# Softmax on one core: eight transfers of 3 to 25 rows in place of ten, five-row scaling of the late tiles, a later test for the general path

## The chip, the cores and the metric

One core of one Trainium2 chip. The metric is device time in microseconds, the median of several executions. All executions told of here were in the fast state (granted clock 1.0), so they are compared with each other. Executions of the kernel before agree within 0.3%; the effects below are about 1% or less, so every experiment was timed in five rounds.

## The reference

```
x: [16, 1024, 512] float32
x_scaled = x / 2.0
exp_x = exp(x_scaled - max(x_scaled, axis=-1))
out = exp_x / sum(exp_x, axis=-1)
```

The kernel takes exp without subtracting the maximum and counts afterwards whether every row's sum lies in a safe range. If not, a general path with the maximum runs over all data. For this input it doesn't run, but its test does.

## The kernel before

There are 16384 rows of 512 floats, 128 rows for each partition. A "row" below is one such row in all 128 partitions: 256 KB. Everything works in place in an arena of 98 rows, so the last 30 rows must wait until stores have freed room. ScalarE issues loads, SyncE issues stores.

```python
TILES = [(3, 0), (5, 3), (15, 8), (15, 23), (15, 38), (15, 53), (15, 68), (15, 83), (15, 0), (15, 15)]  # rows, place
LATE = {8: (0, 1, 2), 9: (3,)}   # tile 8 waits for the stores of 0, 1, 2; tile 9 for that of 3
TURN = 83                        # ScalarE issues the late loads after the exps of 83 rows
...
# VectorE: chunks of five rows, two together where a tile has two left
for j, ks in enumerate(pairs):
    nc.vector.reciprocal(...)._wait_ge(s_exp, ks[-1] + 1).then_inc(s_rec, 1)
    nc.vector.tensor_mul(...)._wait_ge(s_rec, j + 1).then_inc(s_mul, 1)
...
# SyncE: a store waits for the last scaling of its tile
def store(eng, t):
    eng.wait_ge(s_mul, upto[t])
    eng.dma_start(out=dram(of, t), in_=sb(t)).then_inc(stored_by.get(t, s_end), 16)
...
# VectorE, ScalarE and GpSimd: the test for the general path
def rounds(eng, body, step=1):
    eng.wait_ge(s_flag, 1)
    eng.reg_load(i, flag[0:1, 0:1])
    with eng.While(lambda: eng.snap(i, ...) < last):
        body(...)
```

Of the kernel before, what the change touches and what calls it, by code (L numbers as in the profile page):

```python
# [6 lines left out]



TILES = [  # L10
    (3, 0), (5, 3), (15, 8), (15, 23), (15, 38), (15, 53), (15, 68), (15, 83), (15, 0), (15, 15),
]

LATE = {8: (0, 1, 2), 9: (3,)}
ARENA = 98

HEAD = [3]
# [1 line left out]

SPREAD = 1  # L20

TURN = 83

LO, HI = 1.0, 1.0e30
G = 8


@with_exitstack
def kernel(
# [5 lines left out]
    nc = tc.nc  # L35
# [3 lines left out]
    Exp = mybir.ActivationFunctionType.Exp  # L39
# [3 lines left out]
    of = out.flatten_outer_dims()  # L43
    N, D = xf.shape
    P = nc.NUM_PARTITIONS
    n_rows = N // P
    assert sum(r for r, _ in TILES) == n_rows

    arena = nc.alloc_sbuf_tensor("arena", (P, ARENA, D), fp32)
# [5 lines left out]
    flag = nc.alloc_sbuf_tensor("flag", (1, 1), mybir.dt.int32)  # L55
    g_max = nc.alloc_sbuf_tensor("g_max", (P, G), fp32)
    g_sum = nc.alloc_sbuf_tensor("g_sum", (P, G), fp32)
    total = nc.alloc_psum_tensor("total", (1, 1), fp32)

    tiles, base = [], 0  # L60
    for r, at in TILES:
        assert at == base % ARENA
# [3 lines left out]
    def dram(ap, t):  # L66
        b, r, _ = tiles[t]
        return ap[b * P : (b + r) * P].rearrange("(p r) d -> p r d", r=r)

    def sb(t):  # L70
        _, r, at = tiles[t]
        return arena[:, at : at + r, :]
# [5 lines left out]
    owner = [max(t for t, (b, _, _) in enumerate(tiles) if b <= s) for s in starts]  # L78
# [2 lines left out]

    pairs = []
    for k, t in enumerate(owner):
        if pairs and len(pairs[-1]) == 1 and owner[pairs[-1][0]] == t:
            pairs[-1].append(k)
        else:
            pairs.append([k])
    upto = [1 + max(j for j, ks in enumerate(pairs) if owner[ks[0]] == t) for t in range(len(tiles))]

    ld = [nc.alloc_semaphore(f"ld{t}") for t in range(len(tiles))]  # L90
    s_home = {t: nc.alloc_semaphore(f"s_home{t}") for t in LATE}
    s_end = nc.alloc_semaphore("s_end")
    s_exp = nc.alloc_semaphore("s_exp")
    s_go = nc.alloc_semaphore("s_go")
# [10 lines left out]
    g_exp = nc.alloc_semaphore("g_exp")  # L105
# [3 lines left out]
    def load(eng, t):  # L109
        r = tiles[t][1]  # L110
        parts = [(0, P, 0, r)]
        if t == SPREAD:
            parts = [(0, P, 0, r - 1), (0, 126, r - 1, r), (126, P, r - 1, r)]
        for p, q, lo, hi in parts:
            eng.dma_start(
                out=sb(t)[p:q, lo:hi], in_=dram(xf, t)[p:q, lo:hi]
            ).then_inc(ld[t], 16)

    stored_by = {u: s_home[t] for t, us in LATE.items() for u in us}
    for t, (_, r, at) in enumerate(tiles):  # L120
        over = {u for u, (_, ru, au) in enumerate(tiles[:t]) if at < au + ru and au < at + r}
        assert over <= {u for v, us in LATE.items() if v <= t for u in us}

    def landings(ts):
        return 16 * len(list(ts))

    at_end = landings(t for t in range(len(tiles)) if t not in stored_by)

    def store(eng, t):
        eng.wait_ge(s_mul, upto[t])  # L130
        eng.dma_start(out=dram(of, t), in_=sb(t)).then_inc(stored_by.get(t, s_end), 16)

    def take(eng, sem, n):
        eng.wait_ge(sem, n).then_inc(sem, -n)  # L134

    def rounds(eng, body, step=1):



        last = n_rows // G  # L140
        i = eng.alloc_register("tile")
        eng.wait_ge(s_flag, 1)
        eng.reg_load(i, flag[0:1, 0:1])
        with eng.While(lambda: eng.snap(i, min_val=0, max_val=last) < last):
            body(eng.snap(i, min_val=0, max_val=last - 1))
            eng.reg_add(i, i, step)
# [5 lines left out]
    def loads():  # L152
        for t in range(2, min(LATE)):
            load(nc.scalar, t)

    def program():

        nc.vector.memset(ones[:, :], 1.0).then_inc(s_ones, 1)  # L158
        for j, ks in enumerate(pairs):
            b, c = starts[ks[0]], sum(sizes[k] for k in ks)  # L160
            a = b % ARENA
            nc.vector.reciprocal(  # L162
                out=recip[:, b : b + c], in_=stats[:, b : b + c]
            )._wait_ge(s_exp, ks[-1] + 1).then_inc(s_rec, 1)
            nc.vector.tensor_mul(  # L165
                out=arena[:, a : a + c],
                in0=arena[:, a : a + c],
                in1=recip[:, b : b + c].unsqueeze(2).to_broadcast([P, c, D]),
            )._wait_ge(s_rec, j + 1).then_inc(s_mul, 1)
        nc.vector.tensor_scalar(  # L170
            out=inside[:, :], in0=stats[:, :], scalar1=LO, scalar2=HI,
            op0=Alu.max, op1=Alu.min,
        ).then_inc(s_cnt, 1)
        nc.vector.tensor_tensor(  # L174
            out=inside[:, :], in0=inside[:, :], in1=stats[:, :], op=Alu.is_equal
        )._wait_ge(s_cnt, 1).then_inc(s_cnt, 1)
        nc.vector.reduce_sum(  # L177
            out=count[:, :], in_=inside[:, :], axis=mybir.AxisListType.X
        )._wait_ge(s_cnt, 2).then_inc(s_cnt, 1)
        nc.vector.tensor_scalar(  # L180
            out=flag[:, :], in0=total[:, :], scalar1=float(N), scalar2=float(n_rows // G),
            op0=Alu.is_ge, op1=Alu.mult,
        )._wait_ge(s_tot, 1).then_inc(s_flag, 1)


        for t in range(len(tiles)):
            nc.tensor.wait_ge(ld[t], 48 if t == SPREAD else 16).then_inc(s_go, owner.count(t))
        nc.tensor.wait_ge(s_ones, 1)
        nc.tensor.matmul(  # L189
            total[:, :], lhsT=count[:, :], rhs=ones[:, :], start=True, stop=True  # L190
        )._wait_ge(s_cnt, 3).then_inc(s_tot, 1)

        nc.scalar.preload_act_table(Exp)  # L193
        for k, c in enumerate(HEAD):
            take(nc.scalar, s_go, 1)
            for b in range(starts[k], starts[k] + c):
                ins = nc.scalar.activation(  # L197
                    out=arena[:, b], in_=arena[:, b], func=Exp, scale=0.5,
                    accum_out=stats[:, b : b + 1],
                )  # L200
            ins.then_inc(s_exp, 1)
        exponentials(straight, TURN)
        for t, us in LATE.items():
            nc.scalar.wait_ge(s_home[t], landings(us))
            load(nc.scalar, t)
        exponentials(TURN, n_rows)

        for t in range(len(tiles)):
            store(nc.sync, t)



        x_g = xf.rearrange("(t p r) d -> t p r d", p=P, r=G)
        o_g = of.rearrange("(t p r) d -> t p r d", p=P, r=G)
        data = arena[:, 0:G]

        def vector(i):
            take(nc.vector, g_go, 1)
            nc.vector.reduce_max(
                out=g_max[:, :], in_=data, axis=mybir.AxisListType.X, negate=True  # L220
            ).then_inc(g_rec, 1)
            take(nc.vector, g_rec, 1)
            nc.vector.tensor_scalar_mul(
                out=g_max[:, :], in0=g_max[:, :], scalar1=0.5
            ).then_inc(g_neg, 1)
            take(nc.vector, g_exp, 1)
            nc.vector.reciprocal(out=g_sum[:, :], in_=g_sum[:, :]).then_inc(g_rec, 1)
            take(nc.vector, g_rec, 1)
            nc.vector.tensor_mul(
                out=data, in0=data, in1=g_sum[:, :].unsqueeze(2).to_broadcast([P, G, D])  # L230
            ).then_inc(g_mul, 1)

        def scalar(i):
            take(nc.scalar, g_neg, 1)
            for r in range(G):
                ins = nc.scalar.activation(
                    out=arena[:, r], in_=arena[:, r], func=Exp, scale=0.5,
                    bias=g_max[:, r : r + 1], accum_out=g_sum[:, r : r + 1],
                )
            ins.then_inc(g_exp, 1)  # L240

        def gpsimd(_):
            nc.gpsimd.wait_ge(s_end, at_end)
            for i in range(n_rows // G):
                nc.gpsimd.dma_start(out=data, in_=x_g[i]).then_inc(g_ld, 16)
                nc.gpsimd.wait_ge(g_ld, 16 * (i + 1)).then_inc(g_go, 1)
                take(nc.gpsimd, g_mul, 1)
                nc.gpsimd.dma_start(out=o_g[i], in_=data).then_inc(g_st, 16)
                nc.gpsimd.wait_ge(g_st, 16 * (i + 1))

        rounds(nc.vector, vector)
        rounds(nc.scalar, scalar)
        rounds(nc.gpsimd, gpsimd, n_rows // G)
        nc.sync.wait_ge(s_end, at_end)

    def exponentials(first, end):
# [62 lines left out]
```

## Time and profile before

| | before |
|---|---|
| time, median | 161.7 us (161.69 to 161.73) |
| span of the profile | 160.1 us |
| moved | 33.55 MB in, 33.55 MB out |
| ScalarE, VectorE busy | 50%, 47% |
| the two data queues, share of the 16 DMA engines | 98% |
| last store issued, last data, end | 148.86, 159.57, 160.06 us |

How to read it: the DMA engines are busy for 98% of this span and no compute engine for more than 50%, so I took the bytes, at the rate that the packets show, for the floor, and looked for moments without work. The lines that carry this are shown in the prediction. The profile's page gives DMA by slices of 4 us; where fractions of a us matter, I used the trace's record of single packets (one packet is one partition's share of a tile, 30720 bytes for 15 rows). That record names no DMA engine. I joined each packet to the one that had ended at most 14 ns before it, which gives 16 chains, and I call these the engines; two engines whose packets end within a few ns of each other can be swapped by this. When an engine is done with its share of a transfer, the record shows a packet of 4 bytes, called its completion record here (336 in the kernel before: 16 for each transfer but one of two partitions). "Nominal" is the usual time of a packet of its size: 385, 761, 1138, 1514 and 1891 ns for 10240, 20480, 30720, 40960 and 51200 bytes, the medians in the traces of the two kernels. That is about 36.8 ns per 1000 bytes and 8 ns fixed.

Three more measurements that the prediction uses, all of the kernel before. While both queues have packets, an engine mostly takes them in turn: between 45 and 125 us, 990 of 1118 data packets that follow another in a chain belong to the other queue. The last load's data end at 131.56 us in the median of the engines; its completion records end at 132.70, 1.14 us or one 15-row packet later, and each arrives some 0.35 us after that (0.33 to 0.44). VectorE's scaling takes 2825 ns for five rows (128x2560) and 5492 ns for ten (128x5120).

### The profile page before, as it was taken

The page shows a single profiled execution, that of the slowest core. Times are in us where ns is not written, and L with a number is a line of the kernel's source. Part 1 is how long each engine was busy: PE and PEld are TensorE (multiplying, and loading weights), DVE is VectorE, ACT ScalarE, POOL GpSimd, SP SyncE. Part 2 cuts the span into 40 slices and gives each one's busy share as a digit, 9 for nine tenths or more (in the row PEclk, how much of TensorE's full clock was granted, in tenths as well). Part 3 has the DMA queues.
Part 4 walks back from the last instruction along what each step waited for, and adds up shares of the span by engine and source line. Part 5 has one row for each costly group of instructions (what it writes and reads, how often), then busy time and mean ns, then how long its engine had stood idle before and what let it go on. Part 6 is the DMA issues. An engine that isn't in the chain of part 4 may idle for free. (4 is left out here: it accounts for less than half of the span.)

```text
span 160.1 us, 666 instructions
## 1 busy us (share of the span) xinstructions
PE 0.2 (0%) x2; PEld 0.1 (0%) x2; DVE 74.9 (47%) x41; ACT 80.6 (50%) x257; POOL 0.2 (0%) x4
## 2 busy tenths in 40 slices
PE   0000000000000000000000000000000000000000
PEld 0000000000000000000000000000000000000000
DVE  0047009939907940199006950199005960099400
ACT  0590597795399007950299006960099205970000
POOL 0000000000000000000000000000000000000000
DMA  7999998999899999999998989898989899999795
GB/s 262 385 491 392 467 435 344 481 399 463 376 484 392 468 399 461 453 407 461 399 476 384 476 384 484 378 476 384 476 384 491 376 484 392 468 430 430 299 438 248
DMA packets 3026, 67.13 MB, mean 419 GB/s; under 512 B 336, under 2 KB 336, under 8 KB 720
## 3 DMA queue, kind: packets, MB, share of 16 engines
q1 hardware_dynamic: 1584, 34.34, 50.1%
q10 hardware_dynamic: 1440, 32.77, 48.1%
q14 instruction: 2, 0.02, 0.0%
HBM read 33.55 MB, written 33.55 MB: 419 GB/s over the span
## 5 line engine op out<-in xcount | busy, mean ns | idle before, releaser
L268 ACT ACTIVATE arena<-arena x125 | 76.6, 614 | 56.8 <-ACTq L134 56.8
L165 DVE TENSOR_TENSOR arena<-arena,recip 128x2560 f32<-128x2560 f32 (+2 forms) x18 | 71.1, 3951 | 0.6
L162 DVE RECIPROCAL recip<-stats 128x5 f32<-128x5 f32 (+2 forms) x18 | 3.5, 196 | 71.4 <-ACT arena L268 65.2
L268 ACT ACTIVATION_READ_ACCUMULATOR arena<-arena x125 | 23.4, 187 | 0.0
L193 ACT ACT_TABLE_LOAD x1 | 1.3, 1283 | 5.8 <-issue 5.8
L197 ACT ACTIVATE arena<-arena 128x512 f32<-128x512 f32 x3 | 1.9, 618 | 0.0
L158 DVE MEMSET ones<- 128x1 f32 x1 | 0.1, 59 | 2.7 <-PEq L37 2.7
L197 ACT ACTIVATION_READ_ACCUMULATOR arena<-arena 128x1 f32 x3 | 0.6, 186 | 0.0
L189 PE MATMUL total<-ones,count 128*1 128x1 f32 x2 | 0.2, 164 | 149.7 <-DVE count L177 149.7
L174 DVE TENSOR_TENSOR inside<-inside,stats 128x128 f32<-128x128 f32 x1 | 0.3, 292 | 0.0
L177 DVE TENSOR_REDUCE count<-inside 128x1 f32<-128x128 f32 x1 | 0.3, 286 | 0.0
L180 DVE TENSOR_SCALAR flag<-total 1x1 int32<-1x1 f32 x1 | 0.1, 147 | 0.3 <-PE total L189 0.3
L170 DVE TENSOR_SCALAR inside<-stats 128x128 f32<-128x128 f32 x1 | 0.2, 220 | 0.0
L189 PEld LDWEIGHTS total<-ones,count 128*1 128x1 f32 x2 | 0.1, 80 | 149.7 <-DVE count L177 149.7
L303 POOL MEMSET const-bfloat16-1.0<- 128x1 bf16 x1 | 0.1, 101 | 0.0
L303 POOL MEMSET const-uint8-127<- 128x1 uint8 x1 | 0.1, 101 | 0.0
L303 POOL MEMSET const-float32-0.0<- 128x1 f32 x1 | 0.1, 98 | 0.2 <-issue 0.2
L303 POOL MEMSET const-float32-1.0<- 128x1 f32 x1 | 0.1, 98 | 0.0
## 6 DMA issues: line engine op xcount, KB each, us to landing
arena<-in_x_dram ACTq DMA_DIRECT2D x8, 3840.0 KB, 43.5
out_dram<-arena SPq DMA_DIRECT2D x8, 3840.0 KB, 29.8
out_dram<-arena SPq DMA_DIRECT2D x1, 1280.0 KB, 23.6
arena<-in_x_dram ACTq DMA_DIRECT2D x1, 1024.0 KB
arena<-in_x_dram SPq DMA_DIRECT2D x1, 768.0 KB, 5.6
out_dram<-arena SPq DMA_DIRECT2D x1, 768.0 KB, 15.3
arena<-in_x_dram ACTq DMA_DIRECT2D x1, 252.0 KB
arena<-in_x_dram ACTq DMA_DIRECT2D x1, 4.0 KB
```

Of the source, the lines that this page charges most:

```text
L158: nc.vector.memset(ones[:, :], 1.0).then_inc(s_ones, 1)
L162: nc.vector.reciprocal(out=recip[:, b : b + c], in_=stats[:, b : b + c])._wait_ge(s_exp, ks[-1] + 1).then_inc(s_rec, 1)
L165: nc.vector.tensor_mul(out=arena[:, a : a + c], in0=arena[:, a : a + c], in1=recip[:, b : b + c].unsqueeze(2).to_broadcast([P, c, D]),)._w ...
L170: nc.vector.tensor_scalar(out=inside[:, :], in0=stats[:, :], scalar1=LO, scalar2=HI, op0=Alu.max, op1=Alu.min,).then_inc(s_cnt, 1)
L174: nc.vector.tensor_tensor(out=inside[:, :], in0=inside[:, :], in1=stats[:, :], op=Alu.is_equal)._wait_ge(s_cnt, 1).then_inc(s_cnt, 1)
L177: nc.vector.reduce_sum(out=count[:, :], in_=inside[:, :], axis=mybir.AxisListType.X)._wait_ge(s_cnt, 2).then_inc(s_cnt, 1)
L180: nc.vector.tensor_scalar(out=flag[:, :], in0=total[:, :], scalar1=float(N), scalar2=float(n_rows // G), op0=Alu.is_ge, op1=Alu.mult,)._wa ...
L189: nc.tensor.matmul(total[:, :], lhsT=count[:, :], rhs=ones[:, :], start=True, stop=True)._wait_ge(s_cnt, 3).then_inc(s_tot, 1)
L193: nc.scalar.preload_act_table(Exp)
L197: ins = nc.scalar.activation(out=arena[:, b], in_=arena[:, b], func=Exp, scale=0.5, accum_out=stats[:, b : b + 1],)
L268: ins = nc.scalar.activation(out=data, in_=data, func=Exp, scale=0.5, accum_out=stats[:, r : n_rows - E + 1 + r][:, bass.ds(now, 1)],)
L303: nc = _bacc.Bacc("TRN2", target_bir_lowering=False, num_devices=1)
```

## The change

The intent: fewer and larger transfers in the middle; a small last tile, scaled in smaller steps, so that its store is ready early; and a test, with its flag load and its branches, that comes later.

```diff
-TILES = [(3, 0), (5, 3), (15, 8), (15, 23), ..., (15, 83), (15, 0), (15, 15)]
-LATE = {8: (0, 1, 2), 9: (3,)}
+TILES = [(3, 0), (5, 3), (15, 8), (25, 23), (25, 48), (25, 73), (20, 0), (10, 20)]
+LATE = {6: (0, 1, 2), 7: (3,)}
-TURN = 83
+TURN = 73
-G = 8
+G = 64                                   # rows per round of the general path
-        if pairs and len(pairs[-1]) == 1 and owner[pairs[-1][0]] == t:
+        if t not in LATE and pairs and len(pairs[-1]) == 1 and owner[pairs[-1][0]] == t:
...
+    near = len(tiles) - 2                # the last store but one gets its own semaphore
+    sem_of = {**stored_by, near: s_near}
...
 def rounds(eng, body, step=1):
+        eng.wait_ge(s_near, 16)
         eng.wait_ge(s_flag, 1)
...                                       # the general path's exps: a loop of one in place of eight in a row
+        nc.sync.wait_ge(s_near, 16)
         nc.sync.wait_ge(s_end, at_end)
```

More of the change, by code (lines that the diff above doesn't have):

```diff
@@ L6 @@
 from concourse._compat import with_exitstack
-TILES = [
-    (3, 0), (5, 3), (15, 8), (15, 23), (15, 38), (15, 53), (15, 68), (15, 83), (15, 0), (15, 15),
-]
-LATE = {8: (0, 1, 2), 9: (3,)}
+TILES = [(3, 0), (5, 3), (15, 8), (25, 23), (25, 48), (25, 73), (20, 0), (10, 20)]
+LATE = {6: (0, 1, 2), 7: (3,)}
 ARENA = 98
@@ L91 @@
     s_home = {t: nc.alloc_semaphore(f"s_home{t}") for t in LATE}
+    s_near = nc.alloc_semaphore("s_near")
     s_end = nc.alloc_semaphore("s_end")
@@ L125, in landings @@
         return 16 * len(list(ts))
-    at_end = landings(t for t in range(len(tiles)) if t not in stored_by)
+    near = len(tiles) - 2
+    sem_of = {**stored_by, near: s_near}
+    at_end = landings(t for t in range(len(tiles)) if t not in sem_of)
     def store(eng, t):
         eng.wait_ge(s_mul, upto[t])
-        eng.dma_start(out=dram(of, t), in_=sb(t)).then_inc(stored_by.get(t, s_end), 16)
+        eng.dma_start(out=dram(of, t), in_=sb(t)).then_inc(sem_of.get(t, s_end), 16)
     def take(eng, sem, n):
@@ L225, in vector @@
             ).then_inc(g_neg, 1)
-            take(nc.vector, g_exp, 1)
+            take(nc.vector, g_exp, G)
             nc.vector.reciprocal(out=g_sum[:, :], in_=g_sum[:, :]).then_inc(g_rec, 1)
@@ L231, in vector, with scalar @@
             ).then_inc(g_mul, 1)
-        def scalar(i):
+        def scalar(_):
             take(nc.scalar, g_neg, 1)
-            for r in range(G):
-                ins = nc.scalar.activation(
-                    out=arena[:, r], in_=arena[:, r], func=Exp, scale=0.5,
-                    bias=g_max[:, r : r + 1], accum_out=g_sum[:, r : r + 1],
-                )
-            ins.then_inc(g_exp, 1)
+            row = nc.scalar.alloc_register("g_row")
+            nc.scalar.reg_mov(row, 0)
+            with nc.scalar.While(lambda: nc.scalar.snap(row, min_val=0, max_val=G) < G):
+                now = nc.scalar.snap(row, min_val=0, max_val=G - 1)
+                nc.scalar.activation(
+                    out=data[:, bass.ds(now, 1)], in_=data[:, bass.ds(now, 1)], func=Exp,
+                    scale=0.5, bias=g_max[:, bass.ds(now, 1)], accum_out=g_sum[:, bass.ds(now, 1)],
+                ).then_inc(g_exp, 1)
+                nc.scalar.reg_add(row, row, 1)
         def gpsimd(_):
```

## The prediction

> **What bounds the kernel now.** I read the page first, then the transfers, the waits, and the timeline of the last 30 us. The page:
>
> ```profile
> span 160.1 us, 666 instructions
> PE 0.2 (0%) x2; PEld 0.1 (0%) x2; DVE 74.9 (47%) x41; ACT 80.6 (50%) x257; POOL 0.2 (0%) x4
> DMA  7999998999899999999998989898989899999795
> GB/s 262 385 491 392 467 435 344 481 399 463 376 484 392 468 399 461 453 407 461 399 476 384 476 384 484 378 476 384 476 384 491 376 484 392 468 430 430 299 438 248
> q1 hardware_dynamic: 1584, 34.34, 50.1%
> q10 hardware_dynamic: 1440, 32.77, 48.1%
> HBM read 33.55 MB, written 33.55 MB: 419 GB/s over the span
> ```
>
> No compute engine is busy for more than half of the span; the two queues' packets together take 98% of the 16 DMA engines. So transfers bound the kernel, and only moments when a DMA engine has nothing to move can be won. Three stand out in the slices: the first two (262, 385), the third from the end (299), and the last (248). The waits say how much slack compute has:
>
> ```profile
> SPq L131 <- DVE arena L165: 143.1, 10, 18.1
> SPq L254 <- DMA out_dram<-arena: 10.8, 1, 10.8
> ```
>
> ```profile
> ACT arena L268 <- ACTq L134: 56.8, 8, 9.1
> ```
>
> ScalarE waits for loads (56.8 us), SyncE for VectorE before each store, and finally 10.8 us for the last store alone. The timeline of the last tile (duration in the second column; a releaser in brackets):
>
> ```profile
> 133.88 0.63 ACT L268 ACTIVATE arena<-arena  x1 [8.85 <-ACTq L134]
> ...
> 140.13 0.22 DVE L162 RECIPROCAL recip<-stats 128x10 f32<-128x10 f32 x1 [9.44 <-ACT arena L268]
> 140.38 5.49 DVE L165 TENSOR_TENSOR arena<-arena,recip 128x5120 f32<-128x5120 f32 x1
> ...
> 145.79 0.18 DVE L162 RECIPROCAL recip<-stats 128x5 f32<-128x5 f32 x1
> 146.01 2.83 DVE L165 TENSOR_TENSOR arena<-arena,recip 128x2560 f32<-128x2560 f32 x1
> ```
>
> The last tile's exps start at 133.88 and VectorE is done with it at 148.84, 14.96 us later. The trace's record of single packets gives the rest: the store before the last ends on the 16 DMA engines between 148.44 and 149.01, and the first packets of the last store start only at 149.69 to 149.84. That is the dip to 299. From there 15 engines finish by 158.99; the sixteenth carries one 8192-byte packet of the instruction queue at 156.90 and ends at 159.56. The span ends with it.
>
> [...]one 15-row packet (30720 B, one partition) takes 1138 ns, so eight on each of 16 engines take 9.10 us for 3.93 MB, or 432 GB/s. The kernel already runs at it[...].
> [...]with both queues full, a 15-row store comes every 18.2 us, 16 x 1138 ns; so larger load packets slow the small stores beside them, but no bandwidth is lost.
> [...]The branches past the general path run at 151.2 to 151.3 here and a fetch lands 5.6 us later, behind data packets; that they belong together is my inference.
> [...]the trace has 2825 and 5492. So two five-row scalings cost 0.16 us more than one ten-row, plus one reciprocal of 0.18 us.
>
> **The change part by part.**
> 1. Fewer, larger transfers: 8 tiles for 10, so 2 loads and 2 stores fewer, 8 packets each per engine: 32 packets. A packet of 10240 B takes 385 ns and one of 30720 B 1138 ns: 36.8 ns per KB (of 1000 B) and about 8 ns fixed. Saved: 32 x 8 = 0.26 us. Estimated packets: 25 rows 1.89 us, 20 rows 1.51, 10 rows 0.76.
> 2. Gap before the last store. Data end of the last load to landing costs up to one packet of the other queue plus about 0.35; in the trace 131.95 to 133.54. Then 10 rows of exp at 0.61 us are 6.1 (15 rows before), and the second five-row scaling ends 3.0 after that. So the last tile takes about 9.5 us in place of 14.96, once ScalarE is free. I laid both queues out packet by packet with the times above: the last load ends near 125, ScalarE frees itself from the 20-row tile near 130, the last store is issued near 142, and the 20-row store before it runs until about 152.4. There is 10 us of slack, and no gap. Gain: 158.99 - (149.01 + 8 x 1.14) = 0.85 us. Five-row scaling of the late tiles costs VectorE 3 x 0.34 us beside transfers, and worth nothing here, given this slack.
> 3. General path. G = 64 shrinks GpSimd's listing from 43 rows to 15: 16 load-store pairs become 2. [...]the 0.57 us (159.56 - 158.99) are won. The later test (after the 20-row store's landing, near 152.7) costs a flag load of 1.07 to 1.12 us on three engines, over near 154, beside a last store that runs to 158.5. SyncE's extra wait is already satisfied, and the trace has 17 ns for such an instruction.
> 4. A new wait. ScalarE now issues the 10-row load only when the 25-row store of tile 3 has landed, and tile 5's exps come behind it. Tile 5 has landed near 80, but tile 3's store, alternating with load packets, lands near 102 in my layout. From there to tile 5's store: issue 0.4, exps and scaling of 25 rows 21.1 (first four chunks of exps 12.3, then 5.74 for the pair and 3.0 for the last five), 0.83 from issue to data: 22.4 us. The DMA has left without that store: tile 4's store (15.1), the 10-row load (6.1), and the end of the 20-row load; in the layout until 125.1, or 23.3 us. It just suffices: cost 0, with 0.9 us of margin.
> Start-up is untouched: tiles of 3, 5, 15 rows as before.
> Sum: 0.26 + 0.85 + 0.57 = 1.68 us, so 160.0. I take off for item 3's inference about 30% of 0.57 and for item 4 little: 160.2.
>
> **The rivals.**
> A. The wait of item 4 overflows. If tile 3's store lands late or the 10-row load passes tile 4's store, the queues run dry near 124 and every us over the margin costs a us. For it: 0.9 us is thin. Against it: what delays that landing are packets, and those move data too. With 1 or 2 us of drying up, 161 to 162. The profile would show a slice well below 400 near 124.
> B. The fetch stays, or moves to the end: the test runs near 154, and 5.6 us later is 159.6, after the data. Then an engine rather than SyncE finishes last: 160.7 to 161.3. For it: the delay before. Against it: GpSimd's code shrinks, and the loop on ScalarE too has one exp in place of eight.
> C. Large transfers move at a higher rate and the time falls by more than 2%, under 158.5. Against it: 16 engines are already 98% busy, and the fixed part of a packet is 8 ns.
> D. 51200-byte rows go slower, or are cut into smaller packets. A cut into two costs 8 ns a time; a slowdown of 1% in 25-row packets alone would cost 0.9 us (six such transfers of 15.1 us). The rise from 10240 to 30720 B speaks against it.
>
> **Range and chances.** Median 160.2 us. The floor is set by bytes: from about 7.6 us on, with every engine busy, 248 row transfers of 0.605 us are left, 150 us, plus packets' fixed 0.9, landing and spread 0.5: 159.0 of span at most, 158.5 at least; the timed run is 1.6 above the span, so 160.1 to 160.6. Range 159.7 to 161.3. Faster by over 2% needs 158.5, which these bytes don't allow: 0.02. Slower needs 164.9, four us of dry queues or a 3% slower rate: 0.03. Within 2%: 0.95.
>
> **What would show each step.** Right: the slice of 299 is gone and the last ten slices but the last stay near 430; SyncE's wait for the last store is longer than 10.8 us, because it is issued long before its turn; one ScalarE wait of some 20 us stands before tile 5's exps; the last packets end within 0.6 us of each other, and no instruction packet lies in the last store; span about 158.6. Wrong: low slices near 124 (rival A), an instruction packet in the last 5 us (B), 25-row packets off 1.89 us (C, D). If the last store's first packet follows its predecessor at once and the time is still above 161.3, my reading of the end is wrong.

## The result, and the profile after

160.30 us (160.17 to 160.48, 4 runs) against 161.69 us (161.64 to 161.73, 4 runs) of the kernel before beside it; ratio 0.9915, 95% interval 0.9897 to 0.9932. Ratios here are the mean time of one kernel's fast runs over that of the other's in the same rounds, so not quite the ratio of the medians. The result is correct. The profiled span went from 160.1 to 158.9 us. So 1.2 us were won within the span, and some 0.2 behind it: each run has its span on record, and time minus span has a mean of 1.36 us in the four runs of the changed kernel and of 1.59 (1.40 to 1.71) in those of the kernel before that are beside the first eight experiments.

The page of the changed kernel: span, DMA share and GB/s in 40 slices, and the two data queues.

```profile
span 158.9 us, 665 instructions
DMA  7999999799699998999999898997999999999996
GB/s 267 392 487 419 487 462 439 304 477 495 294 410 459 454 510 351 438 428 412 425 480 456 371 552 356 397 541 340 449 418 405 505 412 412 412 454 402 464 387 275
q1 hardware_dynamic: 1296, 34.34, 50.5%
q10 hardware_dynamic: 1152, 32.77, 48.4%
```

The 299 near the end is gone. Larger packets make the slices uneven (304, 552, 340), because a slice takes a packet's bytes where it starts; that isn't idle time (from 8 to 156 us the packet records leave the engines without work for less than 0.03 us per slice). The waits of SyncE and of ScalarE:

```profile
SPq L132 <- DVE arena L167: 135.6, 8, 45.3
SPq L260 <- DMA out_dram<-arena: 17.8, 1, 17.8
```

```profile
ACT arena L274 <- ACTq L135: 50.6, 5, 30.3
```

The last store is now issued 17.8 us before the end, 10.8 before: it stands in the queue behind its predecessor. The one wait of 30.3 us is ScalarE behind the store of tile 3. The timeline around it (the 28.37 us are from the first late load's issue to the end of the second's):

```profile
72.92 28.37 ACTq L114 DMA_DIRECT2D arena<-in_x_dram  x2
...
101.81 0.63 ACT L274 ACTIVATE arena<-arena  x1 [30.26 <-ACTq L135]
```

And the last scalings, now of five rows:

```profile
134.86 2.83 DVE L167 TENSOR_TENSOR arena<-arena,recip 128x2560 f32<-128x2560 f32 x1
...
137.82 2.83 DVE L167 TENSOR_TENSOR arena<-arena,recip 128x2560 f32<-128x2560 f32 x1
```

In the packet records the last store is issued at 140.67; its first packet follows its predecessor's on each engine at once (151.49 to 152.37). The 16 engines end between 157.58 and 158.44. In the kernel before, 15 ended within 0.13 us (158.86 to 158.99) and one at 159.57.

### The profile page after: what moved, and what is told of

It is laid out like the page before. It is cut to its first block, busy times and chain, and to the rows that moved or that the text cites. A ratio compares the mean times of both kernels' runs of the same rounds, so it can differ in the third digit from the quotient of the medians.

```text
span 158.9 us, 665 instructions
## 1 busy us (share of the span) xinstructions
PE 0.2 (0%) x2; PEld 0.1 (0%) x2; DVE 75.1 (47%) x43; ACT 80.3 (51%) x257; POOL 0.2 (0%) x4
```

## The experiments

Names that start with b are the kernel before with an edit, those with a the changed kernel or its tiles.

| kernel | median us (range, runs) | ratio to before |
|---|---|---|
| before, beside the first eight | 161.63 (161.49 to 161.79, 12) | 1 |
| before, beside the last four (a_pair2, a_best, a_nopath, after2; another chip) | 161.63 (161.53 to 161.90, 11) | 1 |
| b_five: five-row scaling of the late tiles alone | 160.25 (160.06 to 160.66, 4) | 0.9911 |
| a_tiles: the tile sizes alone | 160.43 (160.15 to 161.06, 6) | 0.9935 |
| b_tail: the change, middle tiles back at 15 rows | 160.38 (160.32 to 160.68, 5) | 0.9927 |
| a_pair, a_pair2: the change without five-row scaling | 159.78 (159.72 to 160.38, 4); 160.39 (159.66 to 161.39, 6) | 0.9885; 0.9921 |
| a_order: the last load after tile 5's exps | 160.35 (160.23 to 161.01, 6) | 0.9934 |
| a_best: a_pair and a_order together | 160.77 (159.79 to 161.08, 6) | 0.9928 |
| a_early: the change with the early test | 160.62 (159.95 to 161.70, 6) | 0.9939 |
| b_nopath: before without the general path | 160.88 (160.72 to 160.94, 4) | 0.9951 |
| a_nopath: the change without the general path | 160.08 (159.83 to 161.21, 6) | 0.9925 |
| b_endtest: before, test after all stores | 162.73 (162.69 to 162.80, 4) | 1.0069 |
| after2: the change again | 160.36 (160.22 to 160.38, 5) | 0.9920 |

Time minus span has a mean of 1.32 to 1.37 us in every version of this table but three: the kernel before (1.59), a_tiles (1.75) and b_endtest (2.64). So about 0.2 us of a gain over the kernel before can lie behind the span, where packets before its end explain nothing. In the kernel before, one more instruction packet starts there (161.39); whether it makes the 0.2 us was not tested.

### b_five: one part alone

```diff
 # in the kernel before, tiles as they were
-        if pairs and len(pairs[-1]) == 1 and owner[pairs[-1][0]] == t:
+        if t not in LATE and pairs and len(pairs[-1]) == 1 and owner[pairs[-1][0]] == t:
```

> The kernel before, with only the late two tiles scaled by five rows; ten tiles, early test. Theory 1 (the gain is won at the end): the last store is issued 2.7 us earlier, near 146.2, so the gap of about 0.85 us before it closes; the instruction packet still falls into the last store and makes one DMA engine some 0.6 us late: 160.8 us. Rival (the gain comes from the larger middle transfers): 161.7 us.

Measured: 160.25 us, as much as the whole change from one line, and 0.5 us more than expected. The last scalings and SyncE's wait for the last store:

```profile
143.38 0.19 DVE L162 RECIPROCAL recip<-stats 128x5 f32<-128x5 f32 x1
143.60 2.82 DVE L165 TENSOR_TENSOR arena<-arena,recip 128x2560 f32<-128x2560 f32 x1
```

```profile
SPq L254 <- DMA out_dram<-arena: 12.5, 1, 12.5
```

The last scaling ends at 146.42 in place of 148.84, the store is issued at 146.46, and no engine has a gap before it. So the gap closes as expected. Instruction packets still fall into the last store, at 153.25 and 153.55. The engine of the first ends at 158.21. That of the second, whose next data packet took 0.40 us longer than nominal, ends last, at 158.80; all others have ended by 158.23. So in this execution, the slowest of the four (160.66), the packet still costs 0.57 us, as Theory 1 had it.

The price isn't fixed, though. With the gap, all 16 engines began the last store together (149.69 to 149.84), and the one that the packet held up set the end (159.57; the others by 158.99). Without it they begin unevenly (148.35 to 149.16 here), and the packet need not set the end: in the profile of a_tiles, which has no gap either, the engine with the packet (146.87) ends at 157.88, before the last one (157.97). Of the 0.5 us beyond the expectation, some 0.24 lie behind the span (1.35 us against 1.59). The rest would be explained if the packet fell on early engines in the three faster runs (160.06 to 160.31); none of them was profiled, and no run takes the general path out of b_five, so this is not shown.

### a_tiles: another part alone

```diff
 # in the kernel before: TILES, LATE and TURN of the change, and nothing else
```

> The kernel before with only the tile sizes of the change (3, 5, 15, 25, 25, 25, 20, 10): scaling in pairs, early test, old general path. Theory 1 (what counts is that the last store is issued before its predecessor ends, and either part does that): the last store is issued near 143.5, eight us early, no gap; 160.3 to 160.9 us with the scatter of the early test. Rival (the five-row scaling closes the gap, tiles give only the packets' 0.26 us): 161.4 us.

Measured: 160.43 us. The last store is issued at 139.71, the 20-row store before it at 133.58; no gap. The rival falls: here VectorE scales in pairs. The reason is that the last load ends near 124 to 125 rather than at 132, and the last tile has 10 rows, so its whole computation is done while earlier stores still run. Either part alone is enough to close the gap, and they don't add. Within the span the tiles alone win even more than the whole change (spans of 158.4 to 159.3, mean 158.75, against 158.8 to 159.1, mean 158.95); 0.4 us of that are lost again behind the span (1.75 us against 1.36), for a reason that no run tests.

### b_tail: large middle tiles taken back

```diff
-TILES = [..., (15, 8), (25, 23), (25, 48), (25, 73), (20, 0), (10, 20)]
+TILES = [..., (15, 8), (15, 23), (15, 38), (15, 53), (15, 68), (15, 83), (20, 0), (10, 20)]
```

> The changed kernel with the six middle tiles back at 15 rows (3, 5, six of 15, 20, 10), late test and five-row scaling kept. Theory 1: the end is as in the changed kernel, 32 more packets per engine cost 0.26 us, and the wait of up to 1.1 us at 124 is gone because ScalarE doesn't stand behind a 25-row store: 160.0 to 160.5 us. Rival (large middle transfers give the gain): 161.3 us or more.

Measured: 160.38 us, inside the range; against 160.30 and 160.36 of the changed kernel the large middle transfers show no gain that these runs resolve. Engines end between 157.58 and 158.11.

### a_pair and a_pair2: the other part taken back

```diff
-        if t not in LATE and pairs and len(pairs[-1]) == 1 and owner[pairs[-1][0]] == t:
+        if pairs and len(pairs[-1]) == 1 and owner[pairs[-1][0]] == t:
```

> The changed kernel with the late tiles scaled ten rows at a time again. Theory 1 (the 20- and 10-row tiles have 10 us of slack): the last store is issued 2.7 us later, near 143.4, still eight us before its turn, 160.3 us. Rival (five-row scaling is what closes the gap in this version too): a gap before the last store and 161 us or more.

Measured: 159.78 us, where three of four runs were below every run of the changed kernel. The last store was issued at 141.41, still ten us before its turn, so no gap. Half a us better was in neither theory; I repeated it beside the changed kernel.

> The changed kernel with the late tiles scaled ten rows at a time, again, beside the changed kernel. Theory 1: within 0.2 us of the changed kernel. Rival: 0.5 us faster than it, 159.8.

Measured: 160.39 us with runs from 159.66 to 161.39, beside 160.36 for the changed kernel. The 0.5 us did not come back in the median. Yet five of these ten runs lie between 159.66 and 159.79, below all nine of the changed kernel (160.17 at the lowest), so it was more than a lucky draw. What differs is the instruction queue, in the pages of the changed kernel and of a_pair:

```profile
q14 instruction: 2, 0.02, 0.0%
```

```profile
q14 instruction: 1, 0.01, 0.0%
```

The changed kernel has such packets at 106.85 and 157.82. The paired version has only the first, in both its profiles, though its branches run at much the same time (154.14 to 154.24, against 154.01 to 154.12). The edit leaves VectorE six instructions fewer (37 for 43) and shortens no other engine's program; a_order and a_best differ by the same edit and by the same packet. So among these versions a packet follows the test with 43 VectorE instructions and not with 37 (a_tiles, with 37 and the old general path, has one); why was not shown. The section on after2 shows what it can cost. The scaling itself lies in slack.

The records show where a slow execution lost its time: in both profiled ones, one engine's packets around 113 to 116 took 0.09 to 0.24 us longer than nominal, and that engine ended last (158.65, 158.69).

### a_order: the load behind which ScalarE waits

In the profile of the changed kernel tile 5's store is issued at 122.92 and its first packets start at 124.07, the moment the last load's packets end there. On six engines that first packet took 0.12 to 1.10 us more than the nominal 1.89 us, and the engines with the three longest delays ended at 158.25, 158.37 and 158.44, three of the last four.

```diff
 # in words
-exponentials(straight, TURN); issue late loads 6 and 7; exponentials(TURN, n_rows)
+exponentials(straight, 73); issue load 6; exponentials(73, 98); issue load 7; exponentials(98, n_rows)
```

> The changed kernel with the 10-row load issued after the exps of tile 5 instead of before them. Theory 1 (ScalarE's wait for tile 3's store makes tile 5's store come too late): tile 5's store is issued some 20 us earlier, no packet near 124 takes longer than 1.95 us, the engines that ended at 158.25 to 158.44 end up to 0.8 us earlier: 159.7 to 160.2 us. Rival (the long first packets at 124 are what any store pays when it starts beside ending loads): they move with the start of that store, 160.3 us.

Measured: 160.35 us. ScalarE's longest wait fell to 12.1 us:

```profile
ACT arena L275 <- ACTq L135: 52.2, 7, 12.1
```

Tile 5's store is issued at 103.70, no packet near 124 is longer than nominal, and the profiled execution's engines end at 157.40 to 157.99. But the time is not lower. The last completion arrives at 158.85, 0.86 us after the last data; what stands in front of it is told under after2.

### a_early: the test moved back

```diff
 def rounds(eng, body, step=1):
-        eng.wait_ge(s_near, 16)
         eng.wait_ge(s_flag, 1)
 def gpsimd(_):
+            nc.gpsimd.wait_ge(s_near, 16)
             nc.gpsimd.wait_ge(s_end, at_end)
```

> The changed kernel without the late test: the three engines load the flag as soon as it is there, near 142. Theory 1 (the later test is what moves the instruction packet past the data): the packet comes 4 to 6 us after the branch, near 148, inside the 20-row store, one engine is 0.3 to 0.6 us late, and the end moves by 0 to 0.6 according to which engine it is: 160.3 to 160.9 us. Rival (the shorter general path is what removes its cost, the time of the test doesn't matter): no instruction packet in the last 20 us, 160.3 us.

Measured: 160.62 us, from 159.95 to 161.70. The flag loads of GpSimd in this kernel and in the changed one (duration in ns, then first and last start in us):

```profile
L144 POOLq TENSOR_LOAD <-flag x1: 1101/1101/1101, 142.1 to 142.1; - x1
```

```profile
L145 POOLq TENSOR_LOAD <-flag x1: 1130/1130/1130, 152.8 to 152.8; - x1
```

In the profiled execution the instruction packet starts at 149.01, between two data packets that took 0.29 and 0.35 us longer than nominal, on the engine that ended last (158.77). In the changed kernel it starts at 157.82, on an engine that had just finished. So the short general path did not remove the packet, as I had assumed it would; the later test moved it. The median's 0.3 us over the changed kernel lies within the scatter of this version.

### b_nopath: what the test and its packet cost before

```diff
 # in the kernel before
-        rounds(nc.vector, vector)
-        rounds(nc.scalar, scalar)
-        rounds(nc.gpsimd, gpsimd, n_rows // G)
```

> The kernel before without the general path and its test; for this input the result is the same. Theory 1 (the branch past the general path causes the instruction packet in the last store, and that one DMA engine sets the end): the packet at 157 is gone, all 16 engines end within 0.2 us near 158.95, span 159.4 to 159.5, 161.1 us; the gap before the last store stays. Rival (the packet comes by itself, not from the branch): it is still there, 161.7 us.

Measured: 160.88 us, 0.75 us under the kernel before beside it. This kernel has no general path and is for diagnosis only. The queues between 148 and 160 us (packets, MB, share) in the kernel before and in this one:

```profile
q1 hardware_dynamic: 160, 3.93, 76.8%
q14 instruction: 1, 0.01, 0.2%
```

```profile
q1 hardware_dynamic: 161, 3.96, 77.2%
```

The instruction packet is gone, all engines end within 0.16 us of each other (159.03 to 159.19), and the gap before the last store is still there (0.88 to 1.52 us). So the packet comes with the general path and its test (b_endtest below shows it following the branches). Of the 0.75 us, 0.5 lie within the span (160.0 to 160.1 before, 159.4 to 159.6 here): that is the packet's price while the gap stands, where my estimate was 0.57. The rest lies behind the span.

### a_nopath: the same removal after the change

> The changed kernel without the general path and its test; same result for this input. Theory 1 (with the late test the instruction packet comes when its engine is done with data, so it costs little): within 0.3 us of the changed kernel, where the same removal won 0.75 us in the kernel before. Rival (the packet or the test still costs as before): 0.6 us or more faster than the changed kernel.

Measured: 160.08 us against 160.36 for the changed kernel in the same rounds (ratios 0.9925 and 0.9920). The removal that won 0.75 us before now wins nothing in the mean that the runs resolve. But four of its six runs (159.83 to 160.21) are below every run of after2; the other two, at 160.99 and 161.21, show that the scatter has another source than the test.

### b_endtest: the test at the very end

```diff
 # in the kernel before
 def rounds(eng, body, step=1):
+        eng.wait_ge(s_end, at_end)
         eng.wait_ge(s_flag, 1)
```

> The kernel before with the test only when all stores have landed. Theory 1: no instruction packet in the last store, so the data end 0.6 us earlier, near 158.99, but the flag load of 1.1 us and the branch lie behind the end: 162.0 to 162.6 us. Rival (engines other than SyncE may finish late at no cost): 161.1 us.

Measured: 162.73 us, 1.1 us slower than before. The engines end evenly, as in b_nopath (158.82 to 158.99), and SyncE is done at 159.35, but now the flag loads follow:

```profile
L144 ACTq TENSOR_LOAD <-flag x1: 492/492/492, 159.4 to 159.4; - x1
L144 POOLq TENSOR_LOAD <-flag x1: 497/497/497, 159.4 to 159.4; - x1
L144 DVEq TENSOR_LOAD <-flag x1: 544/544/544, 159.4 to 159.4; - x1
```

They took 492 to 544 ns here, with the stores done, and 1067 to 1175 ns in the traces of the kernel before and the changed one, with stores in flight. The branches run at about 160.0, and two instruction packets start at 161.02 and 162.16 (the kernel before has one such packet behind its end, at 161.39). SyncE was done 0.7 us earlier than in the kernel before (160.06), and yet the time is 1.1 us longer: in this run it went on past SyncE's end, so the test can be too late as well as too early. The change's place for it, one 6 us store before the end, lies between.

### after2 and a_best: the last half us

> The changed kernel again, beside the next three on one chip, because the version with paired scaling measured 159.8 in another session. Theory 1 (the scaling of the late tiles lies in slack; engines' uneven finish decides the last half us): within 0.2 us of the paired version, somewhere from 159.8 to 160.4. Rival (five-row scaling itself costs about 0.5 us): 160.3, and the paired one 159.8 again.

Measured: 160.36 us (160.22 to 160.38). In its profiled execution the data end at 158.15 at the latest. The instruction packet starts at 157.48, in front of its engine's completion record, and that completion arrives at 158.84; every other has arrived by 158.49. In a_order (packet 157.50, arrival 158.85) and b_tail (157.62, 158.98) it is the same: the last arrival is 1.35 to 1.36 us after the packet's start and 0.34 to 0.35 us after all others. What holds the completion back behind the packet was not shown. In the first profile of the changed kernel the record went out just ahead of the packet, and the end came from a late engine instead. So in these three profiles the later test still costs some 0.35 us. The times agree: the versions whose profiles have an instruction packet at 157.5 to 157.8 (the changed kernel twice, a_order, b_tail) have no run below 160.17 in 20; those without one there (a_pair, a_pair2, a_best, a_nopath) have ten below 160 in 22. Of these, the paired version differs from the changed kernel by the scaling alone.

> The changed kernel with paired scaling and with the 10-row load issued after tile 5's exps: the two edits that cost nothing so far. Theory 1: no wait near 124 and nothing else moved, 159.7 to 160.3 us, no more than 0.3 from the paired version alone. Rival (waits at 124 decide the end): 0.5 us or more below the paired version.

Measured: 160.77 us (159.79 to 161.08): not better, and no version here beats the changed kernel's median by more than the scatter in a repeat. In the profiled execution one engine again had long packets, the longest 0.57 us over nominal at 121.2, and ended at 159.17 while all others were done by 158.06.

## Why the prediction was right, and where it wasn't

The time, 160.30 us, was 0.1 us from the prediction, and that is partly luck, since two misses cancel: the span was to be about 158.6 us and was 158.9, and the time behind it was taken as 1.6, as in the kernel before, and was 1.36. The sum's gain of 1.68 us, before my discount, was too large: 1.39 us were measured, and 1.27 in the repeat, of which some 0.2 lie behind the span, where the sum expected none. Step by step:

- **Transfers bound the kernel and run at their rate**: right. The estimated packets of 1.89, 1.51 and 0.76 us measured 1891, 1514 and 761 ns; 16 engines with packets of 5 to 25 rows would move 426 to 433 GB/s by these times, and between 8 and 156 us the engines moved 429 GB/s before and 431 after. Larger load packets did slow the small store beside them: the data of the five-row store took 11.3 us beside 15-row loads (25.86 to 37.17) and 16.6 beside 25-row ones (29.12 to 45.71).
- **Item 1, 0.26 us for fewer packets**: not resolved. b_tail, with the packets back, is within 0.1 us of the changed kernel.
- **Item 2, the gap**: right. The last store was issued at 140.67 where I had put 142, and the store before it ended at 152.36 where I had 152.4. "Worth nothing here" for the five-row scaling holds beside the tiles of the change (a_pair2); b_five shows that without them it does the whole work.
- **Item 3, the instruction packet**: the step failed in its cause. I took the shorter general path for the reason, with 30% doubt. The packet stays in the changed kernel and in a_early, which have GpSimd's short listing; it goes in a_pair and a_best, where VectorE's program is shorter. What lowered its cost was the closed gap, after which the engines no longer started the last store in step (0.57 us in the profile of b_five, none in that of a_tiles), and the later test, with which the packet came behind its engine's data (157.82 in the changed kernel).
- **The sum** treated items 2 and 3 as independent. In the measured times they aren't: b_five alone gained 1.38 us, as much as the two terms together (1.42) with the packets still there, and removing the test gains 0.75 us with the gap and nothing in the mean without it. Part of this is that b_five and b_nopath win the same 0.25 us behind the span. And the engines' ends are now spread over 0.9 us, which the sum did not have, and the completion behind an instruction packet is 0.35 us late in some executions.
- **Item 4 and rival A**: the wait exists. Tile 3's store arrived at 100.93 (I had near 102), and ScalarE idled 30.3 us where I wrote "some 20". The margin of 0.9 us was nil in one profiled execution, where six first packets were up to 1.1 us late; in the repeat, where tile 3's store arrived at 99.33 and tile 5's was issued at 121.32, it held. a_order, with the wait cut short, has the same median; as a late completion set its profiled end, this leaves open whether the wait costs something under that.
- **Rival B**: half right. The packet did move to the end, 3.8 us after the branch instead of 5.6; the price was far less than I gave it.

Still open is why one DMA engine falls behind in some executions of versions with 25-row tiles. The packet records lead one step back. In five of the nine profiles (the first of the changed kernel, a_pair, a_pair2, a_best, a_early) one engine's load packet at 45.6 to 45.8 takes 0.77 to 1.16 us longer than nominal (0.52 at most on the others), and another load packet follows it. So this engine starts tile 2's store at 50.3 to 50.7 us, where the other fifteen start it by 48.6, and its share of tile 3's store ends one packet late (99.0 to 99.4; the others by 97.7). Tile 3's store then lands at 100.93 to 101.28; in the other four profiles, which have no such engine, at 99.24 to 99.47. Where ScalarE waits for that landing, tile 5's store goes out at 122.9 to 123.1 in place of 121.2 to 121.4: that took the margin of item 4. The same engine ends last in four of the five profiles and last but one in a_early. Why it falls behind at 45.6, and why it (113 to 121 us) or a store's first packets at 124 have long packets later, was seen but neither made nor removed.

## What to carry to other kernels

In a kernel bound by transfers, look for the moment when every DMA engine waits for the same late instruction. Here it lay before the last store: no data packet started between 149.01 and 149.69 us, then all 16 engines began within 0.15 us of each other, and the one with an instruction packet set the end, 0.58 us after the last of the others (159.57, 158.99). In b_five the store was issued at 146.46, before its predecessor ended; the gap was closed, the engines began over 0.81 us, and one line had won 1.38 us. So the cheapest way to an early store is worth trying before a rearrangement. Don't add up gains that have the same cause: take each part alone, and each part away. And compare spans as well as times: what lies behind the profiled span added some 0.24 us to the gain of b_five and took 0.4 us from that of a_tiles.
